# Adding the last expert's rows to the tokens' sums on TensorE instead of by a scatter

## The chip, the cores and the metric

The kernel runs on one core of a Trainium2 chip. The metric is the device time of one execution in microseconds (us). A core has TensorE (matrix products into the accumulation memory PSUM), VectorE, ScalarE and GpSimd (elementwise work; GpSimd cannot read PSUM in this kernel's use), SyncE (here it only issues DMAs), and DMA queues between SBUF and the DRAM. In profile rows TensorE is PE, its weight loads are PEld, VectorE is DVE, ScalarE is ACT, GpSimd is POOL, SyncE is SP.

## The reference, cut to what matters

One decoder layer on 512 tokens of width 1024: three kinds of attention, an output projection, a first LayerNorm, a mixture of 32 experts with the best 4 a token, and a second LayerNorm. Only the end matters here:

```
x   = layer_norm(alpha * x + mix, ln1_g, ln1_b)
ffn = sum over a token's 4 experts of gate * ((up + 1) * glu) @ w_dn[e] + b_dn[e]
out = layer_norm(alpha * x + ffn, ln2_g, ln2_b)

layer_norm(x) = (x - mean(x)) * rsqrt(var(x) + 1e-5) * g + b
```

All values are fp32.

## The kernel before, in words

The first 370 us compute attention, the first norm and the routing. After that all 32 experts run in turn. An expert's tokens are taken from a list of at most 96 rows, in three groups (g) of 32; a token's row of 1024 is laid out as four quarters (c) on four strips of 32 partitions, so that a tile [128, 768] holds 3 groups of 32 rows by 256 columns, in four quarters.

Loop over experts e = 1 to 32 (line 1145): `gate_up` of expert e in eight steps k, then `down` of expert e - 1, then the activation (`act`) of expert e. Between the steps of `gate_up` other work is put in by a dictionary (`between`): after k = 3, the transposes of the last hidden rows. The weights come through a ring of 18 buffers of 1 MB (`slots`, pools of 7, 6 and 5), fetched by SyncE's queue in a fixed order; a buffer is fetched again when TensorE has read it. A group of rows that an expert does not need is skipped by a branch on TensorE (line 1051).

The rows' way back: the sums of all experts are kept in DRAM, in `accd`, which starts as alpha times the first norm's output plus the down biases. At the end of `down` (lines 1115 to 1124) ScalarE reads PSUM and multiplies each row with its gate (tile `y`), and GpSimd issues three indirect DMAs that add the rows to `accd` at the tokens' places.

After the last expert comes a branch (line 1173) around a loop for experts with more than 96 tokens; it is not taken with these inputs, but every engine must load a value and jump over the loop's body. Then (lines 1215 to 1243) SyncE loads `accd` into `x1all`, four tiles of 128 tokens by 1024, and the second norm works on them: per tile two `bn_stats` of 512 columns, an aggregation and an epsilon on VectorE, a power of -0.5 on GpSimd, and then for each half of 512 columns either two fused operations on VectorE or three on ScalarE, GpSimd and VectorE, as the table `NORM2` says. Each half goes to the output by its own DMA.

The program's order is a wish: a planner at compile time orders each engine's instructions by when it believes them ready; instructions in `keep_in_program_order` stay in their order. Waits between engines are put in by the same layer, from what each instruction reads and writes.

Of the kernel before, what the change touches and what calls it, by code (L numbers as in the profile page):

```python
# [28 lines left out]
G = 3 * NE  # L29
NA = (7, 6, 5)  # L30
NORM1 = ["pp", "vv", "pv", "vv"]
NORM2 = ["vp", "vp", "mv", "vv"]
PRN, PTN = 6, 3
ALPHA = 2.0 ** 0.25
EPS = 1e-5
# [19 lines left out]
def layer(ctx, tc, x, w_in, b_in, sinks, cmp_pe, cmp_w1, cmp_w2, w_out, ln1_g, ln1_b,  # L55
# [876 lines left out]
def moe(ctx, tc, env):  # L932
    nc = tc.nc
    ident, routing, x1all = env["ident"], env["routing"], env["x1all"]
    x1d, accd, fetch, order, wt, state = (env[k] for k in ("x1d", "accd", "fetch", "order", "wt", "state"))
    slots, orow, bpart, bsel = env["slots"], env["orow"], env["bpart"], env["bsel"]
    b_gate_up, b_down, xgb = env["b_gate_up"], env["b_down"], env["xgb"]

    rt = ctx.enter_context(tc.tile_pool(name="rt", bufs=1, side="right", reuse_waits="tile"))
    mk = ctx.enter_context(tc.tile_pool(name="mk", bufs=2, side="right", reuse_waits="tile"))  # L940
    msm = ctx.enter_context(tc.tile_pool(name="msm", bufs=4, side="right", reuse_waits="tile"))
    psg = ctx.enter_context(tc.tile_pool(name="psg", bufs=1, space=PSUM))
    pst = ctx.enter_context(tc.tile_pool(name="pst", bufs=3, space=PSUM))
    nring = len(slots)

    gups = psg.tile([P, NG, 512], FT, name="gu")
# [49 lines left out]
    ixs, gwt = {}, {}  # L996
# [29 lines left out]
    def transposed(src, tag, bufs):  # L1026
        dst = mk.tile([P, 6, P], FT, name=tag, tag=tag, bufs=bufs)
        for a, n in ((0, 4), (4, 2)):
            pt = pst.tile([P, 512], FT, name="tp", tag="tr")
            for u in range(n):  # L1030
                tc.keep_in_program_order(
                    nc.tensor.transpose(pt[:, u * P:(u + 1) * P], src[:, (a + u) * P:(a + u + 1) * P], ident))  # L1032
            nc.scalar.copy(dst[:, a:a + n], pt[:, :n * P].rearrange("p (u q) -> p u q", q=P))  # L1033
        return dst

    def listed(xt, k, g):

        return xt[:, 2 * g + k % 2, SL * (k // 2):SL * (k // 2 + 1)]
# [6 lines left out]
    def groups(more, full, part):  # L1045

        full()
        if more is None:
            part()
        else:  # L1050
            with tc.If(more > 0):  # L1051
                part()
# [38 lines left out]
        nc.vector.scalar_tensor_tensor(ga, up, 1.0, ga, op0=OP.add, op1=OP.mult)  # L1091
        return ga.rearrange("p g f -> p (g f)")

    def down(at, weights, ix, gw, more=None):
# [20 lines left out]
        y = mk.tile([P, 768], FT, name="y", tag="y", bufs=1)  # L1115
        sc = []
        for g in range(NG):
            cs = slice(g * 256, (g + 1) * 256)
            nc.scalar.activation(y[:, cs], ya[:, g, :], AF.Copy, scale=gw[g])  # L1119
            sc.append(nc.gpsimd.indirect_dma_start(out=accd, out_offset=bass.IndirectOffsetOnAxis(ap=ix[g], axis=0),  # L1120
                                                   in_=y[:, cs], in_offset=None, bounds_check=NQ * S - 1,
                                                   oob_is_err=False, compute_op=OP.add))
        for a, b in ((0, 1), (0, 2), (1, 2)):
# [21 lines left out]
    for e in range(1, NE + 1):
        if e < NE:
            at = []
            if e + 2 < NE:
                begin(e + 2)
            more[e] = third(e)  # L1150
            ps = gate_up(xt, ring("gu", e), bsel[:, e:e + 1], more[e],
                         {3: lambda: at.append(transposed(hid, "at", 2))})
            if e + 1 < NE:
                xt = transposed(xgs.pop(e + 1), "xt", 1)
        else:
            at = [transposed(hid, "at", 2)]
        down(at[0], ring("dn", e - 1), ixs[e - 1], gwt[e - 1], more.pop(e - 1, None))
        if e < NE:
            hid = act(ps)

    gb = slots[0].tile([P, 2, D], FT, name="gb2", tag="wring")
    for j, src in enumerate((env["ln2_g"], env["ln2_b"])):
        tc.keep_in_program_order(nc.sync.dma_start(gb[:, j], dram_ap(src, 0, [[0, P], [1, D]])))
    g2, b2 = gb[:, 0], gb[:, 1]
# [8 lines left out]
    with tc.If(some > 0):  # L1173
        with tc.For_i(0, NE) as e:
# [43 lines left out]
    norms = []  # L1218
    for t in range(NT):
        x1 = x1all[:, t, :]  # L1220
        mv = msm.tile([P, 2], FT, name="mv", tag="mv")
        st = msm.tile([P, 2, 6], FT, name="bnst", tag="bnst")
        for a in range(2):
            nc.vector.bn_stats(st[:, a, :], x1[:, a * 512:(a + 1) * 512])
        nc.vector.bn_aggr(mv, st)  # L1225
        rs = msm.tile([P, 2], FT, name="rs", tag="rs")
        nc.vector.tensor_scalar(rs[:, 0:1], mv[:, 1:2], EPS, None, op0=OP.add)  # L1227
        nc.gpsimd.tensor_tensor(rs[:, 0:1], rs[:, 0:1], routing.mhalf, op=OP.pow)  # L1228
        if "v" * 2 != NORM2[t]:
            nc.vector.scalar_tensor_tensor(rs[:, 1:2], mv[:, 0:1], -1.0, rs[:, 0:1], op0=OP.mult, op1=OP.mult)  # L1230
        norms.append((mv, rs))
    for t, (mv, rs) in enumerate(norms):
        for a in range(2):
            cs = slice(a * 512, (a + 1) * 512)
            v = x1all[:, t, cs]
            if NORM2[t][a] == "v":
                nc.vector.scalar_tensor_tensor(v, v, mv[:, 0:1], g2[:, cs], op0=OP.subtract, op1=OP.mult)  # L1237
                nc.vector.scalar_tensor_tensor(v, v, rs[:, 0:1], b2[:, cs], op0=OP.mult, op1=OP.add)  # L1238
            else:
                nc.scalar.activation(v, v, AF.Identity, bias=rs[:, 1:2], scale=rs[:, 0:1])  # L1240
                (nc.vector if NORM2[t][a] == "m" else nc.gpsimd).tensor_tensor(v, v, g2[:, cs], op=OP.mult)  # L1241
                nc.gpsimd.tensor_tensor(v, v, b2[:, cs], op=OP.add)  # L1242
            nc.sync.dma_start(orow[t * P:(t + 1) * P, cs], v)


_INS = ['x', 'w_in', 'b_in', 'sinks', 'cmp_pe', 'cmp_w1', 'cmp_w2', 'w_out', 'ln1_g', 'ln1_b', 'router_w',
# [24 lines left out]
```

## Time and profile before

| what | us |
|---|---|
| median of 3 runs (1443.23 to 1447.45) | 1443.6 |
| the profiled execution, in all | 1455.69 |
| its span, from first to last instruction | 1453.9 |
| TensorE busy | 1343.3 (92%) |
| VectorE busy | 408.5 (28%) |
| ScalarE busy | 302.4 (21%) |
| GpSimd busy | 383.3 (26%) |

The page's slices show TensorE busy in nine tenths of nearly every slice until the last one, where it stands still and its granted clock is half; the DMA engines are full from the middle to the slice before the last two. The rows below are from the same profiled execution; their times are counted from the span's start. A row of the timeline gives the start, the duration, the engine, the line, the operation, what it writes and reads, the count, and in brackets how long the engine was idle before it and what ended that.

### The profile page before, as it was taken

The numbers are of one execution on the slowest core, as the hardware profiler recorded it, in microseconds if no ns is written. First come the engines' busy times: TensorE is split into PE (matmuls) and PEld (weight loads), VectorE is DVE, ScalarE is ACT, GpSimd is POOL, SyncE is SP. The second block draws the span as 40 slices with busy tenths as digits, with TensorE's granted clock in tenths as the row PEclk, the third lists the DMA queues.
The fourth block names the chain that finished last, engine by engine and source line by source line (L and its number), as shares of the span: only waits on it lengthen the run. The fifth ranks groups of instructions, "written<-read, shape, count | busy, mean of one in ns | idle before, by whom it ended". The sixth has DMA issues, their size and how long they took to land. (4 is left out here: it accounts for less than half of the span.)

```text
span 1453.9 us, 32160 instructions
## 1 busy us (share of the span) xinstructions
PE 1343.3 (92%) x13949; PEld 701.3 (48%) x13950; DVE 408.5 (28%) x874; ACT 302.4 (21%) x696; POOL 383.3 (26%) x327
## 2 busy tenths in 40 slices
PE   7999899998999998989999998999899999999990
PEld 6777667797334433334343433434344444444440
DVE  3577453636532112123121212121221212111114
ACT  4466255553011111111111111111111111111111
POOL 4422323223113142121212123121212312121124
PEclk9999989999899999999999999999999999999995
DMA  7210121754889999999999999999999999999963
GB/s 194 62 48 1 33 58 44 301 204 169 345 325 362 398 393 403 399 405 408 403 408 391 391 353 398 407 403 404 404 409 404 404 397 407 400 402 400 406 225 122
DMA packets 126115, 453.96 MB, mean 312 GB/s; under 512 B 21326, under 2 KB 53548, under 8 KB 93188
## 3 DMA queue, kind: packets, MB, share of 16 engines
q1 hardware_dynamic: 106372, 430.80, 74.9%
q0 software_dynamic: 18864, 18.72, 5.8%
q8 instruction: 127, 2.08, 0.6%
q10 hardware_dynamic: 720, 2.10, 0.4%
q14 instruction: 32, 0.26, 0.1%
HBM read 440.87 MB, written 18.87 MB: 316 GB/s over the span
## 5 line engine op out<-in xcount | busy, mean ns | idle before, releaser
L1061 PE MATMUL gu<-wring,xt 128*32 128x512 f32 x5120 | 590.3, 601 | 31.3 <-PEq L1051 25.9
L1061 PEld LDWEIGHTS gu<-wring,xt 128*32 128x32 f32 x5120 | 181.0, 111 | 394.4 <-issue 376.7
L1102 PE MATMUL ya<-wring,at 128*32 128x256 f32 x5312 | 315.7, 380 | 10.9 <-issue 3.8
L1120 POOL DMA_INDIRECT accd<-y,ix x96 | 153.1, 1595 | 485.0 <-ACT y L1119 463.6
L1085 DVE TENSOR_SCALAR ga<-gu 128x768 f32<-128x768 f32 x32 | 30.6, 958 | 794.1 <-PE gu L1061 484.6
L1102 PEld LDWEIGHTS ya<-wring,at 128*32 128x32 f32 x5312 | 179.0, 110 | 130.8 <-issue 32.9
L1021 POOL DMA_INDIRECT xg<-x1d,ix x93 | 95.5, 1027 | 320.2 <-issue 242.6
L1119 ACT ACTIVATE y<-ya,gw 128x256 f32<-128x256 f32 x96 | 38.5, 472 | 313.0 <-issue 269.4
L177 POOL TENSOR_TENSOR wl<-raw,wh 128x1024 fp32r<-128x1024 f32 (+2 forms) x28 | 67.8, 2430 | 105.4 <-ACT wh L174 105.4
L1033 ACT COPY xt<-tp 128x512 f32<-128x512 f32 (+1 forms) x62 | 26.7, 481 | 320.9 <-PE tp L1032 272.1
L1033 ACT COPY at<-tp 128x512 f32<-128x512 f32 x64 | 27.5, 482 | 295.2 <-PE tp L1032 287.0
L906 DVE TENSOR_TENSOR places<-slot,pos 128x1536 bf16<-128x1536 bf16 x32 | 55.9, 1750 | 14.9 <-PE ixp L916 14.9
L248 PE MATMUL pjt<-xh,wh 128*128 128x512 f32 (+1 forms) x136 | 54.6, 402 | 0.8 <-DVE xl L226 0.8
L248 PE MATMUL pjt<-xh,wl 128*128 128x512 f32 (+1 forms) x136 | 54.4, 400 | 0.0
L248 PE MATMUL pjt<-xl,wh 128*128 128x512 f32 (+1 forms) x136 | 54.1, 398 | 0.0
L174 ACT CAST wh<-raw 128x1024 fp32r<-128x1024 f32 (+2 forms) x28 | 29.5, 1053 | 52.3 <-issue 26.1
L1032 PEld LDWEIGHTS tp<-ident,ga 128*128 128x128 f32 x192 | 20.4, 140 | 31.1 <-PEq L1051 15.6
L434 ACT ACTIVATE pr<-pr,nm 128x256 f32<-128x256 f32 (+3 forms) x64 | 33.7, 528 | 7.6 <-DVE nm L433 7.0
L1032 PEld LDWEIGHTS tp<-ident,xg 128*128 128x128 f32 x186 | 19.8, 141 | 29.5 <-issue 17.6
L1090 DVE TENSOR_TENSOR ga<-ga,sg 128x768 f32<-128x768 f32 x32 | 30.6, 956 | 9.7 <-ACT sg L1089 9.5
L1061 PE MATMUL gu<-bpart,bsel 96*32 96x512 bf16 x332 | 30.3, 386 | 2.3 <-ACT xg L725 1.5
L1032 PE MATMUL tp<-ident,ga 128*128 128x128 f32 x192 | 27.6, 280 | 4.2 <-PEq L1051 4.2
(319 smaller groups left out, 1390.7 us busy)
## 6 DMA issues: line engine op xcount, KB each, us to landing
wring<-in_w_gate_up_dram SPq DMA_DIRECT2D x256, 1024.0 KB
wring<-in_w_down_dram SPq DMA_DIRECT2D x128, 1024.0 KB
raw<-in_w_in_dram SPq DMA_DIRECT2D x16, 512.0 KB
raw<-in_w_out_dram SPq DMA_DIRECT2D x8, 512.0 KB
x1all<-in_x_dram SPq DMA_DIRECT2D x4, 512.0 KB
x1d<-x1all ACTq DMA_DIRECT2D x4, 512.0 KB
accd<-x1all POOLq DMA_DIRECT2D x4, 512.0 KB
x1all<-accd SPq DMA_DIRECT2D x4, 512.0 KB
```

The costliest lines, as they stand in the source:

```text
L177: eng.tensor_tensor(l[:, :m], raw[:, :m], h[:, :m].bitcast(FT), op=OP.subtract)
L248: nc.tensor.matmul(ps[:, qs], a[:, k, :], b[:, k, qs], start=(k == 0 and n_ == 0), stop=(k == 7 and n_ == 2))
L434: nc.scalar.activation(pr[:, :n], pr[:, :n], AF.Exp, bias=nm, scale=-1.0, accum_out=den)
L906: ins = self.nc.vector.tensor_tensor(a, self.slot[:, None, :].to_broadcast([P, n, NG * P]), pos[:, :, None].to_broadcast([P, n, NG * P]), ...
L1021: nc.gpsimd.indirect_dma_start(out=xg[:, g * 256:(g + 1) * 256], out_offset=None, in_=x1d, in_offset=bass.IndirectOffsetOnAxis(ap=ix[g], a ...
L1032: nc.tensor.transpose(pt[:, u * P:(u + 1) * P], src[:, (a + u) * P:(a + u + 1) * P], ident))
L1033: nc.scalar.copy(dst[:, a:a + n], pt[:, :n * P].rearrange("p (u q) -> p u q", q=P))
L1061: nc.tensor.matmul(ps[SL * c:SL * (c + 1), g, :], lhs(g), w[:, c * 512:(c + 1) * 512], start=start, stop=stop)
L1085: nc.vector.tensor_scalar(ga, v[:, :, :, 0], 7.0, None, op0=OP.min)
L1102: nc.tensor.matmul(ya[SL * c:SL * (c + 1), g, :], listed(at, k, g), w[:, k % 2, c * 256:(c + 1) * 256], start=(k == 0 and g % 2 == 0), sto ...
L1119: nc.scalar.activation(y[:, cs], ya[:, g, :], AF.Copy, scale=gw[g])
L1120: sc.append(nc.gpsimd.indirect_dma_start(out=accd, out_offset=bass.IndirectOffsetOnAxis(ap=ix[g], axis=0), in_=y[:, cs], in_offset=None, b ...
```

## The change

The last expert's rows are not scattered. Instead:

- A new function `last_places` runs after step k = 5 of expert 31's `gate_up`. It builds, for each group g and each tile of 128 tokens t, a matrix `spread` that says which of the list's places belongs to which token: VectorE compares (`places`) and multiplies the identity with the routing mask (`who`), TensorE multiplies the two in bf16 (12 products of 128 columns), ScalarE copies the results into a free ring buffer.
- `down` of expert 31 writes its scaled rows into another ring buffer (`ylast`), and issues no indirect DMA.
- After the branch, the PSUM tiles of the experts are released, and two PSUM tiles of four banks each take the sums: tiles t = 0 and 1 share the four banks of one, t = 2 and 3 those of the other, a quarter c to each bank. TensorE adds the spread rows (12 products of 32 rows by 256 columns a tile) and, by an identity product, the loaded `accd` (4 products of 128 rows).
- The second norm reads these sums in PSUM. Tile 0's statistics are four `bn_stats` on VectorE. For tiles 1 to 3 ScalarE makes them, by two reads of each half with an accumulator (a copy scaled by 1/1024, and a square), and VectorE adds the halves and forms the variance. All of the normalising is two fused operations a half on VectorE, the first reading PSUM. GpSimd only takes the power.

```diff
+    def last_places():
+        a = mk.tile([P, NT, NG * P], BF, name="places", tag="places")
+        routing.places(a, routing.pos[:, NE - 1])
+        for t in range(NT):
+            nc.vector.tensor_tensor(who[:, t], ident, routing.msk[:, t, NE - 1:].to_broadcast([P, P]), op=OP.mult)
+        w = slots[len(order) % nring + 1].tile([P, 2, 1024], FT, name="spread", tag="wring")
...
+        for g in range(NG):
+            pt = pst.tile([P, 512], FT, name="tp", tag="tr")
+            for t in range(NT):
+                tc.keep_in_program_order(nc.tensor.matmul(pt[:, t * P:(t + 1) * P], a[:, t, g * P:(g + 1) * P], who[:, t],
+                                                          start=True, stop=True))
+            nc.scalar.copy(w[:, g], pt.rearrange("p (t q) -> p t q", t=NT))
...
-                         {3: lambda: at.append(transposed(hid, "at", 2))})
+                         {3: lambda: at.append(transposed(hid, "at", 2)),
+                          5: lambda: last_places() if e == NE - 1 else None})
...
-    gb = slots[0].tile([P, 2, D], FT, name="gb2", tag="wring")
+    gb = slots[len(order) % nring].tile([P, 2, D], FT, name="gb2", tag="wring")
...
+    banks.close()
+    psf = ctx.enter_context(tc.tile_pool(name="psf", bufs=1, space=PSUM, reuse_waits="tile"))
+    pair = [psf.tile([P, NQ, 512], FT, name=f"sums{a}") for a in range(2)]
+    sums = [pair[t // 2][:, :, t % 2 * 256:(t % 2 + 1) * 256] for t in range(NT)]
...
     for t in range(NT):
+        for g in range(NG):
+            for c in range(NQ):
+                r = slice(SL * c, SL * (c + 1))
+                nc.tensor.matmul(sums[t][:, c, :], spread[0][r, g, t, :], ylast[0][r, g * 256:(g + 1) * 256],
+                                 start=(g == t % 2 == 0), stop=False, skip_group_check=True)
+        for c in range(NQ):
+            nc.tensor.matmul(sums[t][:, c, :], ident, x1q[:, t, c, :], start=False, stop=True, skip_group_check=True)
+        if t == 0:
+            for c in range(NQ):
+                nc.vector.bn_stats(st[:, c, :], sums[t][:, c, :])
+            nc.vector.bn_aggr(mv[:, 0], st)
+            nc.vector.tensor_scalar(mv[:, 0, 1:2], mv[:, 0, 1:2], EPS, None, op0=OP.add)
+        else:
+            for a in range(2):
+                h = slice(2 * a, 2 * a + 2)
+                nc.scalar.activation(x1q[:, t, h], sums[t][:, h], AF.Copy, scale=1.0 / D,
+                                     accum_out=part[:, t, 0, a:a + 1])
+                nc.scalar.activation(x1q[:, t, h], sums[t][:, h], AF.Square, scale=D ** -0.5,
+                                     accum_out=part[:, t, 1, a:a + 1])
+            nc.vector.tensor_tensor(mv[:, t, :], part[:, t, :, 0], part[:, t, :, 1], op=OP.add)
...
+        nc.gpsimd.tensor_tensor(mv[:, t, 1:2], mv[:, t, 1:2], routing.mhalf, op=OP.pow)
         for a in range(2):
+            h = slice(2 * a, 2 * a + 2)
+            v = x1q[:, t, h]
+            nc.vector.scalar_tensor_tensor(v, sums[t][:, h], mv[:, t, 0:1], g2[:, h], op0=OP.subtract, op1=OP.mult)
+            nc.vector.scalar_tensor_tensor(v, v, mv[:, t, 1:2], b2[:, h], op0=OP.mult, op1=OP.add)
+            nc.sync.dma_start(orow[t * P:(t + 1) * P, a * S:(a + 1) * S], x1all[:, t, a * S:(a + 1) * S])
```

## Rows read from the trace of the kernel before

**Rows 1.** The chain of waits in order of time: start, length, what.

```profile
1386.67 40.28 DMA accd<-y,ix
```

**Rows 2.** The timeline of the last 40 us.

```profile
1415.65 1.55 POOL L1120 DMA_INDIRECT accd<-y,ix  x1 [0.30 <-issue]
1417.04 3.66 PE L1102 MATMUL ya<-wring,at 128*32 128x256 f32 x64 [0.46 <-PEq L1051]
1420.89 1.20 ACT L1119 ACTIVATE y<-ya,gw 128x256 f32<-128x256 f32 x3 [7.76 <-PEq L1051]
1425.36 1.55 POOL L1120 DMA_INDIRECT accd<-y,ix  x1 [0.30 <-issue]
1428.24 1.76 SPq L1217 DMA_DIRECT2D x1all<-accd  x4
1431.46 1.29 DVE L1224 BATCH_NORM_STATS2 bnst<-x1all 128x6 f32<-128x512 f32 x2 [27.23 <-DMA x1all<-accd]
1433.09 0.74 DVE L1237 SCALAR_TENSOR_TENSOR x1all<-x1all,mv,gb 128x512 f32<-128x512 f32 x1
...
1434.38 1.87 DVE L1224 BATCH_NORM_STATS2 bnst<-x1all 128x6 f32<-128x512 f32 x3
...
1448.32 1.40 DVE L1238 SCALAR_TENSOR_TENSOR x1all<-x1all,rs,gb 128x512 f32<-128x512 f32 x2
```

**Rows 3.** Lines 1172, 1173: count: duration ns min/median/max, first and last start.

```profile
L1172 PEldq TENSOR_LOAD <-nbi x1: 312/312/312, 1420.9 to 1420.9; - x1
...
L1173 PEldq COMPARE_BRANCH  x1: 3375/3375/3375, 1421.3 to 1421.3; - x1
```

**Rows 4.** Windows: length, busy PE, PEld, DVE, ACT, POOL, granted clock, DMA share, GB/s.

```profile
520.00:522.00 2.00, 0.53 (x8) 0.00 (x0) 0.00 (x0) 0.00 (x0) 1.42 (x2) 1.00 0.98 366
...
580.00:582.00 2.00, 2.00 (x15) 0.47 (x11) 0.00 (x0) 0.00 (x0) 1.27 (x1) 0.50 1.06 369
582.00:584.00 2.00, 2.00 (x16) 0.36 (x8) 0.00 (x0) 0.00 (x0) 0.00 (x0) 0.71 1.03 366
584.00:586.00 2.00, 1.67 (x18) 0.92 (x18) 0.00 (x0) 0.78 (x2) 0.00 (x0) 1.00 1.06 373
...
1418.00:1424.00 6.00, 2.69 (x52) 1.63 (x44) 0.00 (x0) 1.20 (x3) 2.05 (x2) 0.90 0.10 9
1424.00:1428.00 4.00, 0.00 (x0) 0.00 (x0) 0.00 (x0) 0.00 (x0) 2.60 (x2) 0.50 0.34 43
```

**Rows 5.** The timeline of TensorE's matmuls, four short stretches.

```profile
390.41 0.70 PE L972 MATMUL ip<-bd,gt 32*128 32x512 f32 x2
...
522.19 1.06 PE L1061 MATMUL gu<-wring,xt 128*32 128x512 f32 x8 [1.66 <-remote]
...
578.11 6.12 PE L1061 MATMUL gu<-wring,xt 128*32 128x512 f32 x32 [4.18 <-PEq L1051]
...
1391.95 0.85 PE L1032 MATMUL tp<-ident,ga 128*128 128x128 f32 x6 [0.32 <-PEq L1051]
```

**Rows 6.** Groups by line and shape: count, busy us, mean ns, idle before.

```profile
L1033 ACT COPY at<-tp 128x512 f32<-128x512 f32 x32 | 18.7, 586 | 295.2 <-PE tp L1032 287.0 <-PEq L1051 8.2
...
L434 ACT ACTIVATION_READ_ACCUMULATOR pr<-pr,nm 128x1 f32 x64 | 12.2, 190 | 0.0
...
L434 ACT ACTIVATE pr<-pr,nm 128x512 f32<-128x512 f32 x10 | 7.2, 722 | 3.4 <-DVE nm L433 3.4
...
L1238 DVE SCALAR_TENSOR_TENSOR x1all<-x1all,rs,gb 128x512 f32<-128x512 f32 x5 | 3.6, 740 | 0.0
...
L1228 POOL TENSOR_TENSOR rs<-rs,mhalf 128x1 f32<-128x1 f32 x4 | 3.5, 885 | 7.4 <-DVE rs L1227 7.4
```

**Rows 7.** The timeline of the output projection, TensorE and then VectorE.

```profile
297.45 0.28 PE L747 MATMUL op<-wh,mfl 128*128 128x256 f32 x1
...
297.76 0.75 DVE L754 SCALAR_TENSOR_TENSOR x1all<-x1all,op 128x256 f32<-128x256 f32 x2 [2.31 <-PE op L747]
```

More of the change, by code (lines that the diff above doesn't have):

```diff
@@ L31 @@
 NORM1 = ["pp", "vv", "pv", "vv"]
-NORM2 = ["vp", "vp", "mv", "vv"]
 PRN, PTN = 6, 3
@@ L941, in moe @@
     msm = ctx.enter_context(tc.tile_pool(name="msm", bufs=4, side="right", reuse_waits="tile"))
-    psg = ctx.enter_context(tc.tile_pool(name="psg", bufs=1, space=PSUM))
-    pst = ctx.enter_context(tc.tile_pool(name="pst", bufs=3, space=PSUM))
+    banks = ExitStack()
+    psg = banks.enter_context(tc.tile_pool(name="psg", bufs=1, space=PSUM, reuse_waits="tile"))
+    pst = banks.enter_context(tc.tile_pool(name="pst", bufs=3, space=PSUM, reuse_waits="tile"))
     nring = len(slots)
@@ L1092, in act, with down @@
         return ga.rearrange("p g f -> p (g f)")
-    def down(at, weights, ix, gw, more=None):
+    def down(at, weights, ix, gw, more=None, y=None):
         ya = yaps
@@ L1114, in down @@
             groups(more, full, lambda: [rows(w, k, range(2, NG)) for k, w in ws.items()])
-        y = mk.tile([P, 768], FT, name="y", tag="y", bufs=1)
+        kept = y is not None
+        if not kept:
+            y = mk.tile([P, 768], FT, name="y", tag="y", bufs=1)
         sc = []
@@ L1119, in down @@
             nc.scalar.activation(y[:, cs], ya[:, g, :], AF.Copy, scale=gw[g])
+            if kept:
+                continue
             sc.append(nc.gpsimd.indirect_dma_start(out=accd, out_offset=bass.IndirectOffsetOnAxis(ap=ix[g], axis=0),
@@ L1122, in down @@
                                                    oob_is_err=False, compute_op=OP.add))
-        for a, b in ((0, 1), (0, 2), (1, 2)):
+        for a, b in () if kept else ((0, 1), (0, 2), (1, 2)):
             tc.declare_no_dep(sc[b].ins, sc[a].ins, reason="a token is in an expert's list once")
@@ L1133, in moe @@
     xgs = {}
+    who = xgb[(NE - 3) % 3].bitcast(BF)[:, :NT * P].rearrange("p (t q) -> p t q", t=NT)
+    spread, ylast = [], []
+    def last_places():
[4 more added lines that the diff above has]
+        w = slots[len(order) % nring + 1].tile([P, 2, 1024], FT, name="spread", tag="wring")
+        w = w.rearrange("p a c -> p (a c)")[:, :NG * NT * P].rearrange("p (g t q) -> p g t q", g=NG, t=NT)
+        for g in range(NG):
[4 more added lines that the diff above has]
+            nc.scalar.copy(w[:, g], pt.rearrange("p (t q) -> p t q", t=NT))
+        spread.append(w)
+        y = slots[len(order) % nring + 2].tile([P, 2, 1024], FT, name="ylast", tag="wring")
+        ylast.append(y.rearrange("p a c -> p (a c)")[:, :768])
     def begin(e):
@@ L1156, in moe @@
             at = [transposed(hid, "at", 2)]
-        down(at[0], ring("dn", e - 1), ixs[e - 1], gwt[e - 1], more.pop(e - 1, None))
+        down(at[0], ring("dn", e - 1), ixs[e - 1], gwt[e - 1], more.pop(e - 1, None), ylast[0] if e == NE else None)
         if e < NE:
             hid = act(ps)
-    gb = slots[0].tile([P, 2, D], FT, name="gb2", tag="wring")
+    gb = slots[len(order) % nring].tile([P, 2, D], FT, name="gb2", tag="wring")
     for j, src in enumerate((env["ln2_g"], env["ln2_b"])):
@@ L1217, in moe @@
         nc.sync.dma_start(x1all[:, t, :], av[t * P:(t + 1) * P, :])
-    norms = []
-    for t in range(NT):
-        x1 = x1all[:, t, :]
-        mv = msm.tile([P, 2], FT, name="mv", tag="mv")
-        st = msm.tile([P, 2, 6], FT, name="bnst", tag="bnst")
-        for a in range(2):
[L1224 to L1243, printed above, removed]
+    banks.close()
@@ new lines, in moe @@
+    psf = ctx.enter_context(tc.tile_pool(name="psf", bufs=1, space=PSUM, reuse_waits="tile"))
+    pair = [psf.tile([P, NQ, 512], FT, name=f"sums{a}") for a in range(2)]
+    sums = [pair[t // 2][:, :, t % 2 * 256:(t % 2 + 1) * 256] for t in range(NT)]
+    st = msm.tile([P, NQ, 6], FT, name="bnst", bufs=1)
+    part = msm.tile([P, NT, 2, 2], FT, name="part", bufs=1)
+    mv = msm.tile([P, NT, 2], FT, name="mv", bufs=1)
+    x1q = x1all.rearrange("p t (c d) -> p t c d", c=NQ)
+    g2, b2 = (v.rearrange("p (c d) -> p c d", c=NQ) for v in (g2, b2))
@@ new lines, in moe @@
+    for t in range(NT):
+        for g in range(NG):
[18 more added lines that the diff above has]
+            nc.vector.tensor_tensor(mv[:, t, :], part[:, t, :, 0], part[:, t, :, 1], op=OP.add)
+            neg = msm.tile([P, 1], FT, name="neg", tag="neg")
+            nc.vector.scalar_tensor_tensor(neg, mv[:, t, 0:1], mv[:, t, 0:1], mv[:, t, 1:2], op0=OP.mult,
+                                           op1=OP.subtract)
+            nc.vector.tensor_scalar(mv[:, t, 1:2], neg, -1.0, EPS, op0=OP.mult, op1=OP.add)
+        nc.gpsimd.tensor_tensor(mv[:, t, 1:2], mv[:, t, 1:2], routing.mhalf, op=OP.pow)
+        for a in range(2):
+            h = slice(2 * a, 2 * a + 2)
[3 more added lines that the diff above has]
+            nc.sync.dma_start(orow[t * P:(t + 1) * P, a * S:(a + 1) * S], x1all[:, t, a * S:(a + 1) * S])
```

## The prediction

> **What bounds the kernel now.** I read the page first, then the chain of waits, then the timeline of the last 40 us, and only then rows of single lines. The page has one wait at the end of its chain: the scatter of the last expert's rows into accd. In the chain in order of time it is the largest piece [rows 1]; its start lies earlier than the change, because a scatter follows the scatters before it. The timeline gives the lengths [rows 2]. TensorE's last matmul ends at 1417.04 + 3.66 = 1420.70. ScalarE scales the rows until 1422.09, GpSimd issues the third scatter until 1426.91, SyncE can load accd from 1428.24, and the first statistic starts at 1431.46: 10.8 us from the last matmul to the first statistic. The norm then takes until 1448.32 + 1.40 = 1449.72, and output, drains and end another 4.2 to the span's 1453.9. So 33.2 us follow the last matmul, and the change acts on these alone, apart from one insertion before them.
>
> **Ahead of the tail: the matrix that spreads the rows.** After k = 5 of expert 31's gate/up TensorE gets 12 bf16 matmuls of 128 columns, ScalarE three copies, VectorE one comparison (places) and four products (who). Six transposes put in after k = 3 held TensorE for 0.85 us, with 0.32 idle ahead of them in place of the usual 0.2 [rows 5]; twelve bf16 products are between that and 0.4 us if they stream faster, 1.6 if each costs what a transpose does (0.14). I take 0.9. TensorE has no idle time left to hide it, so all later times move by 0.9. The copies (three of 586 ns, [rows 6]) and the VectorE work lie where these engines idle (ScalarE's idle row before its last scaling says 7.76 us, [rows 2]): nothing, and at most their own 1.8 us if that cover were gone. The gamma/beta buffer is the same pool's next buffer: nothing.
>
> **Removed.** Three scatters, and the wait of accd's loads for them. Those loads now wait for expert 30's third scatter, issued by 1417.20 [rows 2]; with the 1.3 us that the last one needed from issue to the loads (1426.91 to 1428.24) they start at 1418.5 + 0.9 and the first tile lands 3.2 us later, at 1422.6. That is before TensorE can use it. Also gone are GpSimd's and ScalarE's shares of the second norm.
>
> **What is late next: TensorE's own branch.** In the old kernel nothing follows on TensorE, so its jump over the untaken overflow body was free. Its value load starts at 1420.9 and its branch takes 3375 ns [rows 3]; two semaphore instructions end at 1425.0. The sums are behind that jump: earliest start 1425.1 + 0.9 + 0.1 of waits = 1426.1, while rows and loads are ready by 1423.0. The gap on TensorE is 4.5 us, and that has a second price. The granted clock fell from 2.4 to 1.2 GHz in this very stretch of the old kernel (0.90, then 0.50). After a gap of 4.18 us it was still 0.50 when TensorE had resumed at 578.11, 0.71 on average over 582 to 584 and 1.00 after; so it was low for 5.0 us of work. After a gap of 1.66 us it stayed at 1.00 [rows 4, 5]. I take 5.0 us at half rate.
>
> **The sums.** Per tile: 12 fp32 matmuls with 32 rows each, four row strips, and 4 identity matmuls over 128 rows, all 256 columns wide. In ya, 32 such matmuls in four column strips took 3.66 us, that is 0.457 for four side by side [rows 2]. Row strips do the same if they run together: the two first 32-row matmuls of the bias sum lie within 0.70 us though one lasts 0.68 [rows 5]. So 3 x 0.457 = 1.4, and the identity ones, one after the other, 4 x 0.457 = 1.8: 3.2 us a tile. Bounds: 2.5 (the eight identity instructions at a transpose's 0.14), 7.3 (strips in turn).
> The Trainium skill ("TensorE: Matmul & The Clock Gate", Part 3: Packing small matmuls) measured 3.07 times for four row strips, not four. By it a tile takes 0.4 us more, the sum 1.7 us more; this trace shows two strips side by side, not four.
>
> **Who may touch a bank.** Two tiles share each PSUM bank (0 with 1, 2 with 3). In the output projection VectorE's residual of the first tile of such a pair starts at 297.76, with the end of the second tile's last matmul (issued 297.45), after 2.31 us idle [rows 7]: a read of one half waits for writes to the other. So tile 1's sums should wait until VectorE has read tile 0's, and tile 3's until tile 2's are read. VectorE's order in the old tail shows that instructions are put in order of readiness: the first tile's product (1433.09) stands before the next tile's statistics (1434.38), against the program's order [rows 2]. I take TensorE's order as 0, 2, 1, 3.
>
> **The sum**, by one engine after the other:
> - TensorE: tile 0 gets 2.5 us of work done in the 5.0 slow ones, then 0.7: 1431.8. Tile 2 until 1435.0.
> - VectorE on tile 0: two statistics of 512 took 1.29 [rows 2], four of 256 run bank by bank behind the identity matmuls; with aggregation 1432.4, two products that read PSUM (0.7 each, by 740 ns, [rows 6]) until 1433.8. So tile 1 is not held: 1435.0 to 1438.2.
> - ScalarE on tile 2: four reads of 512. A PSUM copy of that size is 586 ns; with the accumulator 722 + 190 from SBUF, overlapping; 0.65 each is my value between 0.5 and 0.9. It starts when two of four banks are done, 1434.1, to 1436.7. Three small VectorE operations 0.4, two products: 1438.5.
> - TensorE tile 3: 1438.5 to 1441.7; ScalarE 1440.8 to 1443.4; 0.4; four products 2.8 (the power, 885 ns on GpSimd, lies beside the first two); hand-overs 0.7: 1447.3. VectorE's others fit between.
> - End: + 4.2 = 1451.5, against 1453.9: **2.4 us less**.
> That execution took 1455.69 in all, 1.8 more than its span, and 12.1 more than the median of the runs, 1443.6. The tail is latencies, so I carry the difference over whole: 1443.6 - 2.4 = 1441.2, with 1438.5 to 1443.5 for this case by the bounds of ScalarE's reads (+-1.2), the insertion (-0.5, +0.7) and the clock (-1).
>
> **Rivals.**
> 1. Tiles summed in the program's order 0, 1, 2, 3 with the bank waits: tile 1 waits to 1433.8, to 1437.0; tile 2 to 1440.2, its statistics to 1441.9, products 1443.7, tile 3 to 1446.9, ScalarE 1448.6, end 1456.7: +2.8, 1446.4. For it: the bank row. Against: the order by readiness. The Trainium skill ("PSUM — Partial Sum Buffer", PSUM bank collisions raise a hardware error) says that two engines on one bank at once is an error, reads included, so software must keep them apart; by that rule the waits are certain and this order is the price of packing two tiles in a bank. The trace agrees as far as [rows 7] go. Chance 0.15.
> 2. Slower: the clock stays at 1.2 GHz through all sums, because TensorE works in short bursts. A tile takes 6.4: ends at 1432.5, 1438.9, 1445.3, 1451.7; ScalarE's last pair 1453.0, then 0.4 + 2.8 + 0.7 + 4.2 = 1461.1: +7.2, 1450.8. It decides once the low clock lasts 5 us longer than I took (each us costs half of one). For it: the 0.50 of the old tail. Against: after 578.11 dense work brought it back, and 0, 2, 1 are dense. Chance 0.13.
> 3. Row strips run in turn: 7.3 a tile, four tiles at 1457.8, end 1467.2: +13.3, 1456.9. Against: [rows 5]. Chance 0.05.
> 4. The change does more than I credit: the branch does not hold the sums (its target is now code that goes on), they start at 1423.3 after a gap of 1.7, and the clock stays up, as after the 1.66 gap. Tiles end at 1426.5, 1429.7, 1432.9, 1436.4, ScalarE 1438.1, end 1446.2: -7.7, 1435.9. Against: 3375 ns measured at the same jump. Chance 0.17.
> That the change does not do what it says would show as accd's loads still waiting for a scatter of expert 31; nothing in the diff issues one, no chance given.
>
> **The numbers.** Forecast 0.50, rivals 0.15, 0.13, 0.05, 0.17. What can be told from no change is 0.3%, 4.3 us: faster means below 1439.3, slower above 1447.9. Faster: rival 4 and 0.14 of the forecast's low edge, 0.31. Slower: rivals 2, 3 and a third of rival 1, 0.23. Same: 0.46. Range for 8 in 10: 1436 to 1449; beyond it lie rival 3, most of rival 2 and the low half of rival 4.
>
> **What would show it.** In the new tail: a TensorE branch of about 3.4 us between the last ya matmul and the first sums; 0.50 granted for some 5 us of the sums; about 3.2 us a tile after that; TensorE's order 0, 2, 1, 3; ScalarE's four reads of a tile in 2.6 us; accd's loads before 1420. I am wrong if the sums start with the scaled rows (rival 4), if tile 2 waits behind tile 1 (rival 1), or if a tile takes over 6 us throughout.

## The result, and the profile after

The changed kernel takes 1450.1 us (median of 10 runs, 1444.75 to 1455.87), the kernel before 1443.2 beside it (10 runs, 1437.87 to 1448.29): ratio 1.0059, 95% interval 1.004 to 1.0078, so slower by 0.6%. Measured again later, 9 runs against 26, it was 1.006 (1.0031 to 1.0089). The forecast was 1441.2 with 1436 to 1449: the sign and the range were both wrong.

The profiled execution took 1449.4 us, its span 1447.3. Its first 1400 us went some 18 us faster than those of the profiled execution before; executions of the kernel before alone lie between 1430.9 and 1467.5 over all runs here. So what is compared here is the **tail**, from the end of the last ya matmul to the end of the span: 33.2 us before ([rows 2] and the span 1453.9), and now 1447.3 - (1399.69 + 2.58), 45.1 by the unrounded times. These are TensorE's rows of the timeline of the changed kernel, and those of the other engines that set its order (start, length, what, and in brackets the idle time ahead of it with what ended it):

```profile
1377.50 0.83 PE L1154 MATMUL tp<-xg,places 128*128 128x128 bf16 x12 [0.18 <-PEq L1051]
1378.26 2.33 PE L1061 MATMUL gu<-wring,xt 128*32 128x512 f32 x17
...
1399.69 2.58 PE L1103 MATMUL ya<-wring,at 128*32 128x256 f32 x44
1400.62 1.76 SPq L1244 DMA_DIRECT2D x1all<-accd  x4
1402.42 1.20 ACT L1122 ACTIVATE ylast<-ya,gw 128x256 f32<-128x256 f32 x3 [7.72 <-PEq L1051]
1409.69 2.94 PE L1260 MATMUL sums<-ylast,spread 32*128 32x256 f32 x24 [7.41 <-PEq L1200]
1412.56 3.42 PE L1263 MATMUL sums<-x1all,ident 128*128 128x256 f32 x8
1415.91 1.56 PE L1260 MATMUL sums<-ylast,spread 32*128 32x256 f32 x18
1416.02 1.43 DVE L1266 BATCH_NORM_STATS2 bnst<-sums 128x6 f32<-128x256 f32 x4 [30.08 <-PE sums L1263]
1417.88 1.41 DVE L1286 SCALAR_TENSOR_TENSOR x1all<-sums,mv,gb 128x512 f32<-128x512 f32 x2
1419.34 1.58 PE L1260 MATMUL sums<-ylast,spread 32*128 32x256 f32 x24 [1.87 <-DVE x1all L1286]
1420.85 1.99 PE L1263 MATMUL sums<-x1all,ident 128*128 128x256 f32 x8
1422.77 0.71 PE L1260 MATMUL sums<-ylast,spread 32*128 32x256 f32 x6
1423.41 1.99 PE L1263 MATMUL sums<-x1all,ident 128*128 128x256 f32 x8
1425.48 0.59 ACT L1272 ACTIVATE x1all<-sums 128x512 f32<-128x512 f32 x1
1429.08 0.74 DVE L1286 SCALAR_TENSOR_TENSOR x1all<-sums,mv,gb 128x512 f32<-128x512 f32 x1
1429.80 0.74 DVE L1286 SCALAR_TENSOR_TENSOR x1all<-sums,mv,gb 128x512 f32<-128x512 f32 x1
1430.60 2.94 PE L1260 MATMUL sums<-ylast,spread 32*128 32x256 f32 x24 [5.20 <-DVE x1all L1286]
1433.48 3.21 PE L1263 MATMUL sums<-x1all,ident 128*128 128x256 f32 x8
1441.26 1.42 DVE L1287 SCALAR_TENSOR_TENSOR x1all<-x1all,mv,gb 128x512 f32<-128x512 f32 x2
```

Four things are to be seen. The first sums come 7.41 us after the last ya matmul, released by TensorE's own sequencer at line 1200, the jump over the overflow loop. Tile 0 then takes 6.3 us (1409.69 to 1415.98). Of tile 2's first 24 instructions only 18 follow; then TensorE stands 1.87 us, because tile 1 needs the bank from which VectorE still reads tile 0; the other 6 come behind tile 1. And ahead of tile 3 it stands 5.20 us, for VectorE's products of tile 2. The scatters of the last expert are gone, as promised: the loads of accd start 1.65 us before the last ya matmul ends, in [rows 2] 7.5 us behind it.

Windows of the tail (length; busy time of PE, PEld, DVE, ACT, POOL; granted clock; DMA share; GB/s):

```profile
1402.27:1409.70 7.43, 0.02 (x3) 0.04 (x3) 0.00 (x0) 1.20 (x3) 0.00 (x0) 0.70 0.66 261
1409.70:1416.00 6.30, 6.30 (x36) 4.61 (x36) 0.00 (x0) 0.00 (x0) 0.00 (x0) 0.54 0.01 3
1416.00:1419.30 3.30, 1.47 (x18) 1.00 (x18) 3.21 (x9) 0.00 (x0) 0.57 (x1) 1.00 0.00 0
1419.30:1425.40 6.10, 6.06 (x46) 4.31 (x46) 1.31 (x2) 2.46 (x8) 0.00 (x0) 1.00 0.24 89
1425.40:1430.60 5.20, 0.00 (x1) 0.00 (x1) 4.90 (x13) 2.71 (x10) 1.10 (x2) 0.86 0.27 101
1430.60:1436.70 6.10, 6.08 (x32) 4.26 (x32) 1.36 (x2) 0.00 (x0) 0.00 (x0) 0.56 0.23 87
```

The clock goes from 2.4 to 1.2 GHz in the 7.4 us gap, tile 0 runs at 0.54 of the full clock, and the same happens a second time in the 5.2 us ahead of tile 3 (0.56). A tile at the full clock takes 3.5 us (1.58 + 1.99, less their overlap), one at the low clock over 6.

Line 1200 by engine (count, then ns min/median/max):

```profile
L1200 PEldq COMPARE_BRANCH  x1: 6322/6322/6322, 1402.9 to 1402.9; - x1
L1200 ACTq COMPARE_BRANCH  x1: 45/45/45, 1403.0 to 1403.0; - x1
```

The same jump took 3375 ns in [rows 3]. The DMA queues of the changed kernel while the branch is under way, first 1402.9 to 1406.7, then 1406.7 to 1407.7 (packets, MB, share of 16 engines):

```profile
q1 hardware_dynamic: 392, 1.43, 93.9%
...
q1 hardware_dynamic: 63, 0.20, 48.5%
q8 instruction: 1, 0.02, 5.9%
...
```

q8 carries instructions, here one packet of 16 KB. I read it as TensorE's code behind the jump: it comes in each branch of this kind, and in runs 1, 5 and 7, which have no branch, it is missing. It does not appear in the 3.8 us in which the loads of accd keep the DMA engines at 94%; it comes as they run dry. In the kernel before, where the branch began at 1421.3, the code came between 1422.2 and 1423, and no data moved beside it:

```profile
q8 instruction: 1, 0.02, 7.4%
q14 instruction: 1, 0.01, 4.3%
```

### The profile page after: what moved, and what is told of

It reads as the page before. It is cut to its first block, busy times and chain, and to the rows that moved or that the text cites. A ratio compares the mean times of both kernels' runs of the same rounds, so it can differ in the third digit from the quotient of the medians.

```text
span 1447.3 us, 32466 instructions
## 1 busy us (share of the span) xinstructions
PE 1347.6 (93%) x14089; PEld 703.7 (49%) x14090; DVE 408.4 (28%) x880; ACT 308.9 (21%) x720; POOL 370.2 (26%) x319
## 5 line engine op out<-in xcount | busy, mean ns | idle before, releaser
L1103 PE MATMUL ya<-wring,at 128*32 128x256 f32 x5312 | 316.4, 380 | 11.3 <-PEq L1051 4.3
L1125 POOL DMA_INDIRECT accd<-y,ix x93 | 148.4, 1596 | 477.8 <-ACT y L1122 457.0
L433 ACT ACTIVATE pr<-pr,nm 128x256 f32<-128x256 f32 (+3 forms) x64 | 33.8, 529 | 7.5 <-DVE nm L432 6.9
L1091 DVE SCALAR_TENSOR_TENSOR ga<-up,ga 128x768 f32<-128x768 f32 x32 | 30.6, 955 | 0.6
```

The lines of the kernel that those rows point to most:

```text
L433: nc.scalar.activation(pr[:, :n], pr[:, :n], AF.Exp, bias=nm, scale=-1.0, accum_out=den)
```

## The experiments

Theory after the two traces: three costs, each with its own cause. The branch makes a gap, longer than before because its code waits behind the loads that the change moved forward; gaps of this length bring the low clock; and the mixed order of tiles with two tiles to a bank makes VectorE's reads hold TensorE. Rivals: the low clock comes from the short bursts themselves, the branch is long for the code that now stands behind it, or the readers are the bound.

All numbers of this table are from one profiled execution each (us): the tail, TensorE's branch, its gap ahead of the first sum, tile 0 from its first to its last matmul, TensorE's idle time ahead of tile 3, tile 3. The last column is the ratio to the kernel before with its 95% interval. An empty field says that the kernel has no such stretch.

| kernel | tail | branch | gap | tile 0 | ahead of 3 | tile 3 | ratio |
|---|---|---|---|---|---|---|---|
| before | 33.2 | 3.38 | | | | | |
| changed | 45.1 | 6.32 | 7.41 | 6.3 | 5.20 | 6.1 | 1.0059 (1.004-1.0078) |
| changed, again | 42.5 | 5.71 | 6.9 | 5.0 | 5.20 | 5.4 | 1.006 (1.0031-1.0089) |
| 1: no branch | 36.1 | none | 1.40 | 3.5 | 5.20 | 5.9 | 1.001 (0.9988-1.0031) |
| 2: late loads | 42.3 | 3.93 | 5.02 | 6.1 | 5.20 | 6.0 | 1.0054 (1.0029-1.0078) |
| 3: order | 35.9 | 6.44 | 7.54 | 6.1 | 1.19 | 3.5 | 0.9983 (0.9962-1.0005) |
| 4: sums first | 38.9 | 5.95 | 7.09 | 6.3 | 0 | 3.5 | 1.0007 (0.9985-1.0028) |
| 5: before, no branch | 33.8 | none | | | | | 0.9987 (0.9971-1.0004) |
| 6: order, late loads | 32.8 | 3.40 | 4.49 | 6.1 | 1.17 | 3.5 | 0.9968 (0.9949-0.9988) |
| 7: order, no branch | 29.4 | none | 1.41 | 5.3 | 1.20 | 3.5 | 0.9946 (0.9922-0.997) |
| 8: before, pool waits | 34.0 | 3.63 | | | | | 0.9977 (0.9954-1.0001) |
| 9: before, again | 32.8 | 3.83 | | | | | 0.9995 (0.9968-1.0022) |
| 10: copies | 32.6 | 4.01 | 5.16 | 5.5 | 0 | 3.5 | 0.9992 (0.997-1.0014) |

The changed kernel, measured again, was expected with a branch of 6 to 6.5 us and a tail of 44 to 45.5. Both came out shorter (5.71 and 42.5): the branch by 0.6, and tiles 0 and 3 by 1.3 and 0.7, since the clock was back sooner (on average 0.69 and 0.63 over the two tiles). So the tail of the same kernel differs by 2.6 us between two executions, and a difference of that size in the tail alone shows nothing.

**1. The branch taken away.**

```diff
-    some = nc.values_load(nbi[0:1, NE:NE + 1], ...)
-    with tc.If(some > 0):
-        with tc.For_i(0, NE) as e:
...
```

> The loop for experts that have more than 96 tokens is left out, with its value load and its branch; these inputs never enter it. In the changed kernel 45.0 us lie between the last ya matmul and the span's end, 7.4 of them TensorE's gap ahead of the first sum. Theory (the branch makes the gap, and the gap makes the clock fall): the first sum starts with the scaled rows, 1.7 us after the last ya matmul; the clock stays at 2.4 GHz, so tile 0 takes 3.5 us and not 6.3; together 8.5 us earlier, tail 36.5, or up to 1.5 more where the loads of accd, then the last to come, hold tile 0. Tile 3 still waits 5 us for its bank and still runs at 1.2 GHz. Median about 1441.5. Rival A (the clock falls because the sums come in short bursts, not because of the gap): tile 0 stays at 6.3 us, tail 39.3, median 1444.5. Rival B (the loads of accd hold the sums anyway, the branch lies beside them): gap still above 5 us, tail above 42.

The timeline and two of its windows:

```profile
1410.25 1.58 PE L1218 MATMUL sums<-ylast,spread 32*128 32x256 f32 x24 [1.40 <-ACT ylast L1122]
1411.76 1.99 PE L1221 MATMUL sums<-x1all,ident 128*128 128x256 f32 x8
...
1428.37 2.94 PE L1218 MATMUL sums<-ylast,spread 32*128 32x256 f32 x24 [5.20 <-DVE x1all L1244]
```

```profile
1410.25:1413.70 3.45, 3.45 (x35) 2.59 (x35) 0.00 (x0) 0.00 (x0) 0.00 (x0) 1.00 1.00 399
...
1428.37:1434.30 5.93, 5.93 (x32) 4.14 (x32) 1.36 (x2) 0.00 (x0) 0.00 (x0) 0.57 0.23 88
```

The sums now wait for the scaled rows and nothing else, tile 0 has the full clock, and the tail is 9.0 shorter (8.5 expected). Rivals A and B fall. The second low stretch, behind the 5.2 us of tile 3, stays: the clock, at 1.00 over 9.3 us before, falls only in that idle time. The median came out 4 us above the 1441.5 expected, 1445.3; the ratio fell by 0.005, 7 us.

**2. The loads started later.**

```diff
-            nc.scalar.activation(y[:, cs], ya[:, g, :], AF.Copy, scale=gw[g])
+            nc.scalar.activation(y[:, cs], ya[:, g, :], AF.Copy, scale=gw[g],
+                                 accum_out=x1all[:, 0, 0:1] if kept and g == 2 else None)
...
-        nc.sync.dma_start(x1all[:, t, :], av[t * P:(t + 1) * P, :])
+        tc.keep_in_program_order(nc.sync.dma_start(x1all[:, t, :], av[t * P:(t + 1) * P, :]))
```

> The first load of accd is made to wait for ScalarE's last scaled rows (that scaling also writes a sum into x1all, which the load overwrites), the other three follow it on SyncE's queue; so the four loads start at about 1.4 us after the last ya matmul and not 1.7 us ahead of its end. Theory (TensorE's branch takes 6.3 us in place of 3.4 because the transfer that brings its code waits behind the 2 MB of the loads): the code's transfer starts about 1 us after the branch again, the branch takes 3.4 to 3.8 us, the gap 4.5 to 5; tile 0's load lands about 3 us after its issue, just in time; tail 45.0 - 2.7 = 42.3, median about 1447.5. Rival (the branch takes longer because of the code that now stands behind it, whatever the DMA does): branch still 6.3 us, tail 45 or, with the loads late, up to 47; median 1450 to 1452.

The branch, and the queues from 1410.3 to 1411.5, about 1 us after its start:

```profile
L1201 PEldq COMPARE_BRANCH  x1: 3932/3932/3932, 1409.7 to 1409.7; - x1
```

```profile
q8 instruction: 1, 0.02, 7.3%
q1 hardware_dynamic: 1, 0.00, 4.7%
...
```

The code comes early again and the branch takes 3.9 us, with the same code behind it. Over the seven executions that have both the branch and the sums behind it, it took 5.7, 6.0, 6.3 and 6.4 us where the loads run ahead of it, and 3.4, 3.9 and 4.0 where they follow. So the collision is shown by the branch's own length, and the rival falls. The tail was 42.3, as expected, but the unchanged kernel also came to 42.5 once, so the tail does not show it. Nor does the ratio, 1.0054: 2.7 us are 0.2%, the half width of the interval.

**3. The order of the tiles.**

```diff
-    for t in range(NT):
+    for t in (0, 2, 1, 3):
...
+                tc.keep_in_program_order(nc.tensor.matmul(sums[t][:, c, :], ...))
```

> TensorE's order of the tiles is pinned to 0, 2, 1, 3, the order that the prediction assumed; the readers follow in the same order. Branch and gap stay as they are (7.4 us, tile 0 in 6.3 us). Theory (18 of tile 2's 24 instructions stand ahead of tile 1, which waits for its bank, and the rest behind it; so ScalarE and VectorE get tile 2 six us late, tile 3 waits 5.2 us and runs at 1.2 GHz): tile 2 is done 3.5 us after tile 0, tile 1 follows without a stall, tile 3's wait for its bank falls from 5.2 to under 1 us, its clock stays at 2.4 GHz; tail 45.0 - 9 = 36, median about 1441. Rival (the readers are the bound: ScalarE's 2.7 us a tile and VectorE's 3 us of products, so the bank wait moves and stays): tile 3 waits about 3 us whichever way, the clock falls again, tail 42 to 45, median 1447 to 1450.

```profile
1425.62 1.58 PE L1260 MATMUL sums<-ylast,spread 32*128 32x256 f32 x24
...
1429.05 1.58 PE L1260 MATMUL sums<-ylast,spread 32*128 32x256 f32 x24
...
1433.74 1.58 PE L1260 MATMUL sums<-ylast,spread 32*128 32x256 f32 x24 [1.19 <-DVE x1all L1288]
```

Tile 2 stands whole behind tile 0, tile 1 follows without a stall, and tile 3 waits 1.19 us and keeps the full clock (1.58 for its first 24). The tail falls by 9.2 (9 expected) to 35.9 with the branch as long as ever. Of these, 6.6 us are gone from tile 0's end to tile 3's start, and 2.6 from tile 3's clock. The order alone costs as much as the branch with the low clock behind it (9.0 in run 1).

**4. All sums ahead of the readers.**

```diff
-                nc.tensor.matmul(sums[t][:, c, :], ...)
+                tc.keep_in_program_order(nc.tensor.matmul(sums[t][:, c, :], ...))
...
+    for t in range(NT):
         if t == 0:
             for c in range(NQ):
                 nc.vector.bn_stats(st[:, c, :], sums[t][:, c, :])
```

> TensorE sums tiles 0, 1, 2, 3 one behind the other ahead of every reader; no reader stands between two tiles of one bank, so TensorE has no bank wait at all, and the readers of tile 0 wait for tile 1. Theory (waits for banks and the second fall of the clock are what the order costs): tile 0 in 6.3 us at the low clock, the others 3.5 each without idle time: last sum 7.4 + 6.3 + 10.5 = 24.2 us after the last ya matmul (34.4 in the changed kernel); then ScalarE's two tiles of the second pair 5.3, small operations and products 3.2, end 4.6: tail 37, median about 1442. It is a little behind the order 0, 2, 1, 3 because ScalarE and VectorE begin later. Rival (the readers are the bound): tail 41 or more, because nothing of the first pair can be read for another 3.5 us.

```profile
1422.30 0.60 ACT L1275 ACTIVATE x1all<-sums 128x512 f32<-128x512 f32 x1 [18.82 <-DVE x1all L1289]
...
1425.81 0.60 ACT L1275 ACTIVATE x1all<-sums 128x512 f32<-128x512 f32 x1 [0.81 <-PE sums L1264]
...
1430.37 0.60 ACT L1275 ACTIVATE x1all<-sums 128x512 f32<-128x512 f32 x1 [1.86 <-DVE x1all L1289]
```

TensorE ran through as expected (its last sum 23.65 us behind the last ya matmul, 24.2 expected), yet the tail was 38.9, not 37. The last row says why: ScalarE's reads of tile 3 wait 1.86 us for VectorE's reads of tile 2, the other tile of the pair. Its reads of tile 1 wait for those of tile 0 in the same way (first row), but that costs nothing, since ScalarE then stands another 0.81 us for tile 3's sums (second row). The waits keep two readers of a bank apart as they keep a reader and a writer; I had worked out only the latter.

**5, 8, 9. The kernel before, three times.** In 5 the overflow loop is left out, as in 1; in 8 the two PSUM pools get the setting that the change gave them; 9 is the kernel before as it was.

```diff
-    psg = ctx.enter_context(tc.tile_pool(name="psg", bufs=1, space=PSUM))
+    psg = ctx.enter_context(tc.tile_pool(name="psg", bufs=1, space=PSUM, reuse_waits="tile"))
...
```

> The kernel before, with the loop for experts of more than 96 tokens left out, with its value load and branch (these inputs never enter it). Theory (the branch was free there because TensorE had nothing left to do, and became a cost by what the change put behind it): 33.2 us from the last ya matmul to the span's end as before, within 0.5, median within 0.3% of before. Rival (the branch costs something in the old kernel too, on another engine's path): tail shorter by 2 to 3 us, median 0.2% lower.

> The kernel before, with one line of the change alone: the two PSUM pools of the expert loop take the setting for waits on reuse that the change gave them. The order of instructions is the same on every engine. Question: in the profiles the stretch from the router to the last ya matmul is 1055.0 us in the kernel before and 1051.5 to 1053.9 in the changed kernel and its variants, though these hold an insertion of 0.8. Theory (the setting is for the closing of the pools and changes no wait in the loop): stretch 1054 to 1055, ratio 1.000 within 0.2%. Rival (finer waits let TensorE start groups earlier): stretch about 1050, ratio 0.996 to 0.997.

> The kernel before, unchanged, in the place of an experiment. The two variants of it that should change nothing came out at 0.9987 and 0.9977. Theory (a kernel in the place of an experiment reads 0.1 to 0.2% low against the runs of before beside it): ratio 0.998 to 0.999, tail 33 to 34 us. Rival (those two ratios were chance or real): ratio 1.000 within 0.05%.

The tails are 33.8, 34.0 and 32.8, with 33.2 so far: the branch was free in the old kernel. From the last matmul of tile sel, behind the router, to the last ya matmul 5 took 1045.4 us and 8 took 1043.7, on one chip; the pool setting shows no effect beyond that 1.7. The stretches expected for 8 (1050 and more) came from other executions and are no measure: the kernel as it was took 1055.0 in the first profile and 1064.5 in 9. The ratios 0.9987 and 0.9977 stand beside 0.9995 for the kernel itself, which is the rival of 9, and all three intervals hold 1; a thousandth or two is what these comparisons cannot tell apart. That is also about what lies between the two measures of the change: 11.1 us by the traces (tails 45.1 and 42.5 against the mean 33.5 of four, and 0.8 for the insertion), 8.5 by the first ratio, with 5.8 to 11.3 as its interval.

**6. Order and late loads together.** Both diffs, of 2 and 3.

> Two edits at once that act at different places: TensorE's order 0, 2, 1, 3 pinned (tail 35.9 us by itself) and the loads of accd started behind the last scaled rows (2.7 us less by itself). Theory (the two costs add, because one lies ahead of tile 0 and the other behind it): tail 35.9 - 2.7 = 33.2, as long as in the kernel before. The medians so far put the changed kernel 6.9 us above before, with a tail 11.8 longer and an insertion of 0.8, so about 5 us less stands in the rest of the program; if that is no chance of the runs, this kernel is 4 to 5 us faster than before (ratio 0.997); if it is, the ratio is 1.0005. Rival (the loads, started later, now hold tile 1 or 2): tail 34.5 to 36.

```profile
1397.31 2.94 PE L1261 MATMUL sums<-ylast,spread 32*128 32x256 f32 x24 [4.49 <-PEq L1201]
...
1411.46 1.58 PE L1261 MATMUL sums<-ylast,spread 32*128 32x256 f32 x24 [1.17 <-DVE x1all L1289]
```

The two costs add: 32.8 (33.2 expected). This is the change as the prediction described it, gap of 4.5 us included, and it is as long as the tails before: with the insertion of 0.8, nothing gained. The ratio 0.9968 would say 0.3% faster; beside it, on that chip, the two variants 5 and 8 with a tail a microsecond longer stood at 0.9987 and 0.9977. I don't call it faster.

**7. Order without the branch.** Both diffs, of 1 and 3.

> TensorE's order 0, 2, 1, 3 pinned, and the loop for experts of more than 96 tokens left out with its branch (these inputs never enter it). This is the case that the prediction called its rival 4, with the order that it assumed. Theory: no gap but 1.4 us, the clock at 2.4 GHz throughout, 3.5 us a tile: tail 35.9 - 6.1 (gap) - 2.7 (clock in tile 0) = 27.1, 6 us less than in the kernel before, ratio 0.992 to 0.996. Rival (without the gap ScalarE and VectorE become the bound, since they need 2.7 and 3 us a tile and the tiles now come each 3.5 us): tail 29 or more, with TensorE idle over 3 us ahead of tile 3 and the clock down again there.

```profile
1396.28 1.58 PE L1218 MATMUL sums<-ylast,spread 32*128 32x256 f32 x24 [1.41 <-ACT ylast L1122]
1399.62 1.99 PE L1222 MATMUL sums<-x1all,ident 128*128 128x256 f32 x8 [1.77 <-DMA x1all<-accd]
...
1410.11 1.58 PE L1218 MATMUL sums<-ylast,spread 32*128 32x256 f32 x24 [1.20 <-DVE x1all L1246]
```

The clock stays at 1.00 through the last tile, and the tail is 29.4, 2.3 more than the theory's 27.1. That is the rival's number, but not its cause: ahead of tile 3 TensorE waits 1.20 us, as in 3. What is late are the loads of accd, for which TensorE waits 1.77 us in tile 0 and 0.37 in tile 2. They wait for expert 30's last scatter, and these rows show it issued until 1391.65, the loads 4.4 us behind it; in 1 it was issued until 1405.33, and the loads came 2.3 behind it, at 1407.65:

```profile
1390.10 1.55 POOL L1125 DMA_INDIRECT accd<-y,ix  x1 [0.30 <-issue]
...
1396.08 1.76 SPq L1202 DMA_DIRECT2D x1all<-accd  x4
```

Why that scatter took longer to land here stays open; between 1390 and 1396 queue q1 still moved 28 packets beside it, and none in the matching stretch of 1 (1403.5 to 1407.6), but no run tests whether they held it. It is the fastest of all (0.9946, 0.9922 to 0.997), but the loop is needed for other inputs.

**10. Banks free after ScalarE's reads.** On top of both diffs of 6.

```diff
...
-                nc.scalar.activation(x1q[:, t, h], sums[t][:, h], AF.Copy, scale=1.0 / D, ...)
-                nc.scalar.activation(x1q[:, t, h], sums[t][:, h], AF.Square, ...)
+                nc.scalar.activation(x1q[:, t, h], sums[t][:, h], AF.Copy, scale=1.0, ...)
+                nc.scalar.activation(junk, sums[t][:, h], AF.Square, ...)
...
+            nc.vector.tensor_scalar(mv[:, t, 0:1], mv[:, t, 0:1], 1.0 / D, None, op0=OP.mult)
...
-            nc.vector.scalar_tensor_tensor(v, sums[t][:, h], mv[:, t, 0:1], g2[:, h], ...)
+            nc.vector.scalar_tensor_tensor(v, v if t else sums[t][:, h], mv[:, t, 0:1], g2[:, h], ...)
```

> Order 0, 2, 1, 3 and late loads as in the run that joined them, and one edit more: ScalarE's first read of a tile leaves the sums themselves in SBUF (the mean is scaled by a small VectorE operation instead), its second read writes into an unused part of a buffer, and VectorE's products of tiles 1 to 3 read SBUF. So a bank is free after ScalarE's four reads. Theory (tile 3 waits for VectorE's products of tile 2, 1.2 us of idle TensorE): tile 3 starts 0.7 us after ScalarE has read tile 2, about 17.5 us after the last ya matmul in place of 18.6, and the tail falls from 32.8 to 31.5, less 0.15 given back by the small operation; ratio 0.001 lower than that of the joined edits. Rival (VectorE is the bound, its products take 3 us a tile and follow each other): tile 3 starts earlier but its statistics wait, tail 32.5 to 33.

Tile 3 started 17.46 us behind the last ya matmul (17.5 expected) with no idle time ahead; the branch was 0.6 longer than in 6, but tile 0 as much shorter. The tail, 32.6, fell by only 0.2, where 1.3 was expected: the rival came out. VectorE's work on tiles 2, 1 and 3 now follows tile on tile, 3.8 us each (3.2 in 6), and it takes up tile 3 (second row) 0.66 us after ScalarE's last read of it (first row). GpSimd's rows tell most of what made it longer:

```profile
1440.62 0.22 ACT L1278 ACTIVATION_READ_ACCUMULATOR ylast<-sums 128x1 f32 x1
1441.50 0.15 DVE L1280 TENSOR_TENSOR mv<-part 128x2 f32<-128x2 f32 x1
```

```profile
1430.09 0.57 POOL L1287 TENSOR_TENSOR mv<-mv,mhalf 128x1 f32<-128x1 f32 x1 [16.20 <-DVE mv L1272]
1435.39 0.98 POOL L1287 TENSOR_TENSOR mv<-mv,mhalf 128x1 f32<-128x1 f32 x1 [4.73 <-DVE mv L1286]
```

The power beside products that read PSUM takes 0.57, beside products that read SBUF 0.98 (three of the four), and VectorE's second products wait for it. At 0.9992 (0.997 to 1.0014) this is the kernel before to the measurement. No version that keeps the loop beats it clearly. A layout that gives the tiles banks of their own was not tried; in it two of a tile's four row strips would write one bank, and no run here shows what that does.

## Why the prediction was wrong

The tail behind the last ya matmul was forecast at 29.9 us (1451.5 - 1420.7 - 0.9) and is 45.1. The 15.2 us, step by step, forecast against trace:

- **The insertion**: 0.9 forecast, 0.76 measured (1377.50 to 1378.26). Right.
- **The branch holds the sums**: right, and rival 4 wrong. Its size failed: gap 4.5 forecast, 7.41 measured, **2.9 us**. I took 3375 ns over from a trace in which the DMA engines stood nearly idle, and in the section before had worked out that the loads of accd would start some 3 us before the branch (1419.4 against 1422.2). That the code has to come through the same engines was never asked. The Trainium skill ("Runtime: NRT & Kernel Launch", Instruction fetch mechanics) says that a taken branch whose target is outside the loaded pages forces a DMA fetch before the engine goes on; the trace agrees, by one q8 packet of 16 KB in each such branch of TensorE, and adds that this packet waits behind bulk loads. The other four engines' branches over the same loop took 45 to 72 ns.
- **The low clock after the gap**: 5.7 us for tile 0 forecast, 6.3 measured, **0.6**. Right in kind; runs 1 and 7 show that the gap is its cause.
- **TensorE's order 0, 2, 1, 3**: this is the step that failed most. From tile 0's end to tile 3's start 6.7 us were forecast and 14.6 measured, **7.9**. I read from VectorE's order in [rows 2] that instructions are placed by readiness, and made of it an order of whole tiles. What came out is a cut through tile 2: 18 of its 24 first instructions ahead of tile 1, the rest behind it. So tile 2 was whole only at 1425.4, ScalarE read it behind tile 1, VectorE's products of tile 2 stood behind those of tile 1, and tile 3 waited for them. With the forecast order (run 3) the stretch is 8.05 us; the last 1.35 of the error are tiles of 3.5 us in place of 3.2, and a ScalarE that starts when the whole tile is summed and not when two of its banks are (VectorE's statistics of tile 0 do the same: its products begin 1.9 us after the sums, and end 3.3 after them where 2.0 were forecast).
- **Bank sharing**: the rule from [rows 7], which the Trainium skill ("PSUM — Partial Sum Buffer", PSUM bank collisions raise a hardware error) backs, held in every trace read here, and for two readers as well (run 4). I used it for whole tiles in a good order and priced the bad order at +2.8 in rival 1. Rival 1 was the nearest to what happened: its mechanism with another sequence, and without the second fall of the clock. Rival 2's figure, 1450.8, is near the measured 1450.1 by luck: its mechanism, a low clock through all sums, did not happen (1.00 from 1416.0 to 1425.4).
- **Tile 3 at the full clock**: 3.2 forecast, 6.1 measured, **2.9**, a consequence of the 5.2 us ahead of it; gone in run 3.
- **Row strips**: four run side by side, 12 matmuls (24 instructions) in 1.58 us against 1.4 forecast. An estimate by the Trainium skill's 3.07 ("TensorE: Matmul & The Clock Gate", Part 3: Packing small matmuls) would have been 1.8; the measured time lies between. Rival 3 wrong.
- **ScalarE's four reads**: 2.6 forecast, 2.7 measured (1436.72 to 1439.42). Right.
- **The end**: from tile 3's last matmul 9.8 forecast, 10.65 measured, **0.9**, again ScalarE's start.

The sum 2.9 + 0.6 + 7.9 + 2.9 + 0.9 is 15.2. Had the order come out as assumed and the loads not met the branch, the tail is run 6: 32.8, still 2.9 above the forecast, the same as before, and no gain. The range failed because neither miss had its full price in it: the bad order was priced without a second low stretch, the branch without its traffic.

## What to carry to other kernels

When work is put on TensorE behind a jump over a long body, look for the fetch of that jump's code in the trace; bulk loads that start just ahead of it made it wait here. Count the branch with the traffic that will be there, and start the loads behind it (run 2; starting them well before was not tried). When two tiles share PSUM banks, write the order of the matmuls down (pin it) rather than assume what a planner makes of readiness, and follow each bank through all its readers, since the idle stretches that this makes, here of 4.5 us and more, are paid again in clock. A tail made of waits is worth changing only if the new chain is counted engine by engine; here a path of 10.8 us through three scatters was replaced by a gap, four tiles and three hand-overs that, with the loop kept, cost as much at their best.

## What the runs showed of the hardware

- TensorE's jump over the overflow loop took 3.4 to 4.0 us where the four 512 KB loads follow it and 5.7 to 6.4 where they run ahead of it; those of the other engines over the same loop 45 to 72 ns.
- The granted clock fell in TensorE's idle stretches of 4.5 to 7.5 us (on average 0.54 to 0.69 over the tile that followed), and stayed at 1.00 behind those of 1.2, 1.4, 1.8 and 1.9.
- GpSimd's power of 128x1 took 0.55 to 0.57 us while VectorE's products read PSUM, and 0.98 while they read two operands from SBUF. Of the four behind the mean of 885 ns in [rows 6], three ran beside such products (0.99 to 1.01) and one with VectorE idle (0.55). The Trainium skill ("GPSIMD Engine Reference", Specifications) names contention between the two engines where a VectorE instruction has two SBUF inputs; run 10 agrees.
